# Two layers' adaLN modulation moved from VectorE, ScalarE and GpSimd to TensorE, ahead of the feed-forward stage

## The chip, the cores and the metric

The kernel runs on one core of a Trainium2 chip (trn2). The metric is the device time of one execution in microseconds (us), the median of several runs. The engines are TensorE (PE in the rows; PEld are its weight loads), VectorE (DVE), ScalarE (ACT), GpSimd (POOL) and SyncE (SP), which here only issues DMAs.

## What is computed

A first block (x is 256 tokens by 1024) mixes a gated delta rule with a dilated attention and has a gated feed-forward; a second block has two layers of attention and a mixture of 16 experts, each modulated by adaLN. All is float32. What the change touches is the modulation:

```python
def second_block(x, c, ada_w, ada_b, ...):
    silu_c = jax.nn.silu(c)                       # c: [1, 1024]
    for i in range(2):
        mod = silu_c @ ada_w[i] + ada_b[i]        # ada_w[i]: [1024, 6144]
        sh1, sc1, g1, sh2, sc2, g2 = [m[:, None, :] for m in jnp.split(mod, 6, axis=-1)]
        h = rms_norm(x, norm_mix_g[i]) * (1.0 + sc1) + sh1
        ...
        x = x + g1 * y
        h = rms_norm(x, norm_ffn_g[i]) * (1.0 + sc2) + sh2
        x = x + g2 * grouped_moe(h, ...)
```

So each layer multiplies one row of 1024 by a matrix of 1024 by 6144: 25 MB of weights a layer, and every weight is used once. It depends on c alone and not on x.

## The kernel before

**Stages.** In program order: the input projection and the gated delta rule, with the dilated attention's projections and heads as filler (the first 180 us or so), the output projection `mix` (L993) and a norm; the feed-forward in 22 steps f of 128 features (L1069 on); the second block's first attention, its experts, the second attention, its experts.

**Products.** Most weights are split into two float32r halves (`subs`, L338; the split is L232: a cast on ScalarE, a subtraction on VectorE or GpSimd), and each product is three float32r matmuls (`feat`, L543, and `tok_half`, L559 to L561). The experts (L1544, L1581), the delta rule's small products (L917 for the doubling, 64 by 64 blocks; L959) and the modulation's sums are in plain float32; the trace shows each of these matmuls as two records.

**Weights.** They come in units of [128, 2048] float32 (1.05 MB) through SP's queue (`wload`, L287). They go in turn to the buffers of up to three rings: `wp` (4 units), `wp2` (3, opened at L1013, where the delta rule's activations were) and `wp3` (3, opened behind the feed-forward, L1111, where the modulation's buffers were).

**Modulation.** `ada_unit(n)` (L365) takes one of 48 units: half the rows of 512 columns. It loads the unit to one of two buffers `wa` (L369); VectorE multiplies three of the four blocks of 128 rows by the column of silu(c) and adds them up in `acc` (L376, L381), and the fourth goes over ScalarE (L378) and GpSimd (L379). After every second unit `ada_sum` (L387) sums `acc` over the partitions with four matmuls against 32 columns of ones (L393), one for each group of 32 output partitions, adds the bias for the gates (L396), copies the row out (L398) and writes it to DRAM. `ada_load`, `ada_finish` and `ada_gate` (L414 to L432) read it back in the feed-forward and later.

**Order.** Each engine works off its own queue in order. The scheduler of the framework sets that order from the program, its priorities and pinned places. Units of modulation are put in by hand: `fill` (L709) advances the filler by one step and the modulation by `more` units at some 30 places of the delta rule, and each feed-forward step takes `step` units more (L1066, L1086), so that 20 units lie before the feed-forward and 28 within it.

```python
    def fill(n=1, more=1.0):
        for _ in range(n):
            drained[0] += 1
            next(filler, None)
            ada(more)
```

Of the kernel before, what the change touches and what calls it, by code (L numbers as in the profile page):

```python
# [10 lines left out]
F32 = mybir.dt.float32  # L11
# [16 lines left out]
# columns of the packed per-partition parameters  # L28
# [7 lines left out]
# columns of the packed rows that every partition gets  # L36
ROW = {"alog": (0, 4), "dtb": (4, 8), "rb": (8, 24), "lam": (24, 280)}
NROW = 280
# columns of the shape constants
# [7 lines left out]
# the first block needs those up to here  # L47
# [3 lines left out]
def _constants():  # L51
# [23 lines left out]
    # negated bias of the merged dilated attention: [q, head, (previous block | own block) keys back to front]  # L75
# [8 lines left out]
    # one-hot T5 bucket of rel = key - query, for rel = 127 .. -384  # L84
# [9 lines left out]
def _pack(inp):  # L94
# [6 lines left out]
    def feat(w):  # L101
        """[D, n] -> units of two blocks of 128 columns, each [128, k, 128 columns]"""
        n = w.shape[1]
        return A(w.reshape(KD, 128, n // 256, 2, 128).transpose(2, 1, 3, 0, 4)).reshape(n // 256, 128, 2048)

    def tok(w):
        """[D, n] -> units of 512 columns and half the rows, each [128, 4 k, 512 columns]"""
        n = w.shape[1]
        return A(w.reshape(2, 4, 128, n // 512, 512).transpose(3, 0, 2, 1, 4)).reshape(n // 256, 128, 2048)
# [27 lines left out]
    o["ada_w"] = A(g["ada_w_2"].reshape(2, 2, 4, 128, 12, 512).transpose(0, 4, 1, 3, 2, 5)).reshape(48, 128, 2048)  # L137
# [19 lines left out]
class InOrder:  # L157
    """an engine whose instructions keep their order in the program"""
# [10 lines left out]
def tile_block(ctx: ExitStack, tc: tile.TileContext, a: dict, out: bass.AP, dbg=None):  # L169
# [60 lines left out]
    def split(h, l, i, eng=None):  # L230
        """i = h + l exactly, each of a float32r's width"""
        return A_.copy(h, i), (eng or V).tensor_tensor(l, i, h.bitcast(F32), op=ALU.subtract)  # L232
# [31 lines left out]
    # the tensor engine's clock rises while x is on its way  # L264
# [25 lines left out]
    def wpair(ap, n):  # L290
        """(e, i) -> the i-th 512 columns of a unit for one of two experts; the n-th unit of a layer also finds room where activations were"""
# [30 lines left out]
    def after(i, name):  # L322
        """i is issued behind an instruction of its engine"""
# [3 lines left out]
    # rooms for split halves: s of two tiles of their own, 8 of one where activations are not  # L327
# [10 lines left out]
    def subs(ap, w=None, pinned=False, by=None, behind=None):  # L338
        """a unit of weights, loaded now or already on its way, as two split halves"""
# [21 lines left out]
    csil = const.tile([128, 8], F32, name="csil")  # L361
    adar = [dr.tile([6 * D], F32, name=f"adar{l}") for l in range(2)]
    ada_acc, ada_sums = [None], []

    def ada_unit(n):  # L365
        """half the rows (four blocks) of 512 columns of a layer's modulation, every fourth block on GpSimd"""
        l, s, u = n // 24, n // 2 % 12, n % 2
        w = adap.tile([128, 2048], F32, tag="wa", name="wa", bufs=2)
        nc.sync.dma_start(w, a["ada_w"][n])  # L369
        if u == 0:  # L370
            ada_acc[0] = adap.tile([128, 512], F32, tag="acc", name="acc", bufs=3)
        acc = ada_acc[0]
        for i in range(4):
            wi, k = w[:, i * 512:(i + 1) * 512], 4 * u + i
            if k == 0:
                V.tensor_scalar(acc, wi, csil[:, k:k + 1], None, op0=ALU.mult)  # L376
            elif i == 3:
                A_.activation(wi, wi, AF.Copy, scale=csil[:, k:k + 1])  # L378
                G.tensor_tensor(acc, acc, wi, op=ALU.add)  # L379
            else:  # L380
                V.scalar_tensor_tensor(acc, wi, csil[:, k:k + 1], acc, op0=ALU.mult, op1=ALU.add)  # L381
        if u == 1:
            if len(ada_sums) == 2:
                ada_sums.pop(0)()
            ada_sums.append(lambda: ada_sum(l, s, acc))

    def ada_sum(l, s, acc):  # L387
        """sum over partitions; with the bias for the gates, which are used as rows"""
        p = ps(128)
        gate = s // 2 in (2, 5)  # L390
        for j in range(4):
            o = p[32 * j:32 * j + 32, :]
            mm(o, ones[:, 0:32], acc[:, j * 128:(j + 1) * 128], start=True, stop=not gate)  # L393
            if gate:
                cb = P("adab")[:, l * 48 + s * 4 + j:l * 48 + s * 4 + j + 1]
                mm(o, cb.to_broadcast([128, 32]), ident, start=False, stop=True)  # L396
        sb = adap.tile([128, 128], F32, tag="adasb", name="adasb", bufs=3)
        A_.copy(sb, p)  # L398
        nc.scalar.dma_start(adar[l][s * 512:(s + 1) * 512].rearrange("(j c) -> j c", j=4),
# [5 lines left out]
    def ada(n):  # L405
        """n units more, fractions carried"""
# [12 lines left out]
    def ada_finish(l, t):  # L419
        """shift and scale as columns (the gates, used as rows, have the bias already)"""  # L420
# [15 lines left out]
    def warm(*waits):  # L436
        """holds the tensor engine's clock up through waits; nothing reads the products"""
# [5 lines left out]
    def rsq(o, i, scale):  # L443
        """o = (i * scale + eps) ** -0.5 through the activation tables"""
# [10 lines left out]
    def norm_rows(update=None, column_major=False, between=None, scaled=True):  # L455
        """x after update(b, c) of its [block, half row] pieces, and the rows of x over their root mean square"""
# [1254 lines left out]
```

## Time and profile before

| what | value |
|---|---|
| runs (3) | 1168.49, 1169.7, 1181.19 us |
| median | 1169.7 us |
| profiled execution, first to last instruction (span) | 1168.8 us |
| TensorE, VectorE, ScalarE, GpSimd busy in the span | 1091.2, 668.5, 467.4, 202.3 us |
| HBM read | 347.40 MB, 298 GB/s over the span |

The page gives the profiled execution's time as its span alone; the median of the runs is 0.9 us above it. The records of matmuls overlap one another, since matmuls are pipelined: the distance between two starts says what one costs, its own length does not. The granted clock stands in the stretches as a share of 2.4 GHz.

### The profile page before, as it was taken

Reading aid. Unit: us, or ns where it says so; the run is one execution under the profiler, and the core shown is the slowest. Engines: PE = TensorE matmul, PEld = TensorE weight load, DVE = VectorE, ACT = ScalarE, POOL = GpSimd, SP = SyncE. Lnnn points to the kernel's source line nnn. Section 1 sums busy time; section 2 is a strip of 40 time slices with the busy share of each in tenths; the row PEclk is TensorE's granted clock in tenths of the full one; section 3 lists DMA queues with packets and bytes.
Section 4 is the critical chain, followed back from the end, with each engine's and each line's share of the span. In section 5 each row is a group of like instructions: output and inputs, shape, how many; then the busy total and the mean of one; then the engine's idle time right before and its main releaser. Section 6 shows DMA issues by size and latency. Waiting matters only on the chain. (4 is left out here: it accounts for less than half of the span.)

```text
span 1168.8 us, 16805 instructions
## 1 busy us (share of the span) xinstructions
PE 1091.2 (93%) x6428; PEld 713.0 (61%) x6428; DVE 668.5 (57%) x1283; ACT 467.4 (40%) x942; POOL 202.3 (17%) x156
## 2 busy tenths in 40 slices
PE   8978889899999989999899998898999899999798
PEld 6957677788898868787334434236876544443332
DVE  6999987899999866777322212026656723221212
ACT  5763365655555565667211112016555511110200
POOL 2245543133123242001000000004221100000000
PEclk9999979899999999999999999899999989999999
DMA  8664766777877965356888999998653679899995
GB/s 323 253 252 182 264 246 223 284 285 279 338 284 311 369 247 177 135 200 221 333 349 343 418 422 423 406 421 316 191 184 144 254 305 372 327 424 424 422 419 203
DMA packets 53083, 349.75 MB, mean 299 GB/s; under 512 B 6392, under 2 KB 7192, under 8 KB 13056
## 3 DMA queue, kind: packets, MB, share of 16 engines
q1 hardware_dynamic: 50288, 342.51, 75.2%
q0 software_dynamic: 1792, 5.62, 1.7%
q8 instruction: 55, 0.90, 0.3%
q10 hardware_dynamic: 912, 0.43, 0.1%
q14 instruction: 36, 0.29, 0.1%
HBM read 347.40 MB, written 1.14 MB: 298 GB/s over the span
## 5 line engine op out<-in xcount | busy, mean ns | idle before, releaser
L1544 PE MATMUL pb<-w,XT 128*64 128x512 f32 x864 | 200.1, 609 | 10.3 <-PEq L1504 10.3
L232 DVE TENSOR_TENSOR wl<-w,wh 128x1024 fp32r<-128x1024 f32 x110 | 141.7, 1292 | 40.5 <-ACT wh L232 34.8
L232 ACT CAST wh<-w 128x1024 fp32r<-128x1024 f32 x132 | 137.6, 1044 | 65.5 <-PE pa L560 45.9
L1544 PEld LDWEIGHTS pb<-w,XT 128*64 128x64 f32 x864 | 61.9, 140 | 128.2 <-issue 124.5
L379 POOL TENSOR_TENSOR acc<-acc,wa 128x512 f32<-128x512 f32 x48 | 78.1, 1627 | 204.1 <-DVE acc L381 132.9
L1563 DVE TENSOR_TENSOR he<-he,pb 128x512 f32<-128x512 f32 (+1 forms) x20 | 11.4, 580 | 175.7 <-PE pb L1544 175.7
L381 DVE SCALAR_TENSOR_TENSOR acc<-wa,csil,acc 128x512 f32<-128x512 f32 x120 | 104.0, 867 | 13.4 <-POOL acc L379 8.9
L1581 PE MATMUL pb<-w,heT 128*64 128x512 f32 x480 | 108.1, 597 | 1.5 <-ACT heT L222 1.5
L1562 ACT ACTIVATE he<-pb 128x512 f32<-128x512 f32 (+1 forms) x20 | 10.0, 512 | 209.3 <-PE pb L1544 209.3
L559 PE MATMUL pa<-wh,hh 128*128 128x512 f32 x224 | 91.0, 408 | 2.5 <-ACT hh L532 2.5
L560 PE MATMUL pa<-wh,hl 128*128 128x512 f32 x224 | 88.4, 395 | 3.0 <-POOL hl L530 1.7
L561 PE MATMUL pa<-wl,hh 128*128 128x512 f32 x224 | 88.4, 394 | 0.0
L232 POOL TENSOR_TENSOR wl<-w,wh 128x1024 fp32r<-128x1024 f32 x22 | 54.7, 2488 | 178.3 <-ACT wh L232 139.4
L1584 DVE SCALAR_TENSOR_TENSOR he<-pb,gsl,g 128x512 f32<-128x512 f32 x32 | 24.0, 751 | 96.9 <-PE pb L1581 96.8
L1581 PEld LDWEIGHTS pb<-w,heT 128*64 128x64 f32 x480 | 32.8, 137 | 64.6 <-issue 58.5
L543 PE MATMUL pb<-hh,whl 128*128 128x256 f32 x320 | 62.3, 288 | 0.9 <-DVE gate L1076 0.9
L232 ACT CAST yh<-he 128x512 fp32r<-128x512 f32 x30 | 18.5, 616 | 103.6 <-DVE he L1584 103.6
L378 ACT ACTIVATE wa<-wa,csil 128x512 f32<-128x512 f32 x48 | 34.6, 722 | 58.5 <-DMA wa<-in_ada_w 57.2
L543 PE MATMUL pb<-hh,wh 128*128 128x256 f32 x192 | 55.5, 289 | 1.1 <-DVE hl L236 1.1
L543 PE MATMUL pb<-hl,wh 128*128 128x256 f32 x192 | 55.4, 288 | 0.0
L543 PE MATMUL pb<-hh,wl 128*128 128x256 f32 x192 | 55.2, 288 | 0.0
L543 PEld LDWEIGHTS pb<-hh,whl 128*128 128x128 f32 x320 | 51.3, 192 | 4.0 <-issue 3.4
(455 smaller groups left out, 2352.4 us busy)
## 6 DMA issues: line engine op xcount, KB each, us to landing
w<-in_m_gu SPq DMA_DIRECT2D x108, 1024.0 KB
w<-in_m_dn SPq DMA_DIRECT2D x58, 1024.0 KB
wa<-in_ada_w SPq DMA_DIRECT2D x48, 1024.0 KB
w<-in_w_gu SPq DMA_DIRECT2D x22, 1024.0 KB
w<-in_a_qkv SPq DMA_DIRECT2D x12, 1024.0 KB
wx<-in_m_gu SPq DMA_DIRECT2D x12, 1024.0 KB
w<-in_b_qkv SPq DMA_DIRECT2D x12, 1024.0 KB
w<-in_w_dn SPq DMA_DIRECT2D x11, 1024.0 KB
```

The source lines that it names most:

```text
L232: return A_.copy(h, i), (eng or V).tensor_tensor(l, i, h.bitcast(F32), op=ALU.subtract)
L378: A_.activation(wi, wi, AF.Copy, scale=csil[:, k:k + 1])
L379: G.tensor_tensor(acc, acc, wi, op=ALU.add)
L381: V.scalar_tensor_tensor(acc, wi, csil[:, k:k + 1], acc, op0=ALU.mult, op1=ALU.add)
L543: mm(p, w[:, c], r[:, k, :], start=(n == 0), stop=(n == 3 * KD - 1))
L559: mm(p[b], hh_, wh[:, c], start=(k == k0), stop=False)
L560: mm(p[b], hl_, wh[:, c], start=False, stop=False)
L561: mm(p[b], hh_, wl[:, c], start=False, stop=((k + 1) % KD == k0))
L1544: mm(pu[i][64 * e:64 * e + 64, :], xt[k // 4][:, k % 4, c0 + 64 * e:c0 + 64 * e + 64], w(e, i), start=(k == 0), stop=(k == KD - 1))
L1563: V.tensor_tensor(he[:, cs], he[:, cs], pu[1][:, cs], op=ALU.mult)
L1581: pin(mm(pd[h][64 * e:64 * e + 64, :], heT[:, k, e, :], w(e, i), start=(k == 0), stop=(k == 3)))
L1584: V.scalar_tensor_tensor(he, pd[h], gsl, g2[:, h * 512:(h + 1) * 512], op0=ALU.mult, op1=ALU.mult)
```

## The change

The modulation becomes matmuls. A unit is now 128 rows of 2048 columns, loaded as two halves of 1024 columns into five buffers (together 20 KB a partition, before 16 KB and the accumulators). Four matmuls, one for each 512 columns, multiply it by silu(c) spread over 32 columns and write to the four groups of 32 partitions of one PSUM bank, where eight units add up. Then come the gates' biases, one copy on ScalarE and one write to DRAM for 2048 columns. `fill` takes 1.8 times as many units, all that are left are done at the end of the delta rule, and the feed-forward has none. The third ring `wp3` opens where the second one does, before the last half of `mix`. The host packs `ada_w` in the new layout. All other lines of the diff only drop comments.

```diff
-    o["ada_w"] = A(g["ada_w_2"].reshape(2, 2, 4, 128, 12, 512).transpose(0, 4, 1, 3, 2, 5)).reshape(48, 128, 2048)
+    o["ada_w"] = A(g["ada_w_2"].reshape(2, 8, 128, 3, 2048).transpose(0, 3, 1, 2, 4)).reshape(48, 128, 2048)
...
     def ada_unit(n):
-        l, s, u = n // 24, n // 2 % 12, n % 2
-        w = adap.tile([128, 2048], F32, tag="wa", name="wa", bufs=2)
-        nc.sync.dma_start(w, a["ada_w"][n])
-        if u == 0:
-            ada_acc[0] = adap.tile([128, 512], F32, tag="acc", name="acc", bufs=3)
-        acc = ada_acc[0]
-        for i in range(4):
-            wi, k = w[:, i * 512:(i + 1) * 512], 4 * u + i
-            if k == 0:
-                V.tensor_scalar(acc, wi, csil[:, k:k + 1], None, op0=ALU.mult)
-            elif i == 3:
-                A_.activation(wi, wi, AF.Copy, scale=csil[:, k:k + 1])
-                G.tensor_tensor(acc, acc, wi, op=ALU.add)
-            else:
-                V.scalar_tensor_tensor(acc, wi, csil[:, k:k + 1], acc, op0=ALU.mult, op1=ALU.add)
-        if u == 1:
-            if len(ada_sums) == 2:
-                ada_sums.pop(0)()
-            ada_sums.append(lambda: ada_sum(l, s, acc))
-
-    def ada_sum(l, s, acc):
-        p = ps(128)
-        gate = s // 2 in (2, 5)
+        l, s, k = n // 24, n // 8 % 3, n % 8
+        ws = [adap.tile([128, 1024], F32, tag="wa", name="wa", bufs=5) for _ in range(2)]
+        for i, w in enumerate(ws):
+            nc.sync.dma_start(w, a["ada_w"][n][:, i * 1024:(i + 1) * 1024])
+        if k == 0:
+            ada_acc[0] = ps(512, "pa")
+        p = ada_acc[0]
+        gates = [j for j in range(4) if (4 * s + j) // 2 in (2, 5)]
         for j in range(4):
-            o = p[32 * j:32 * j + 32, :]
-            mm(o, ones[:, 0:32], acc[:, j * 128:(j + 1) * 128], start=True, stop=not gate)
-            if gate:
-                cb = P("adab")[:, l * 48 + s * 4 + j:l * 48 + s * 4 + j + 1]
-                mm(o, cb.to_broadcast([128, 32]), ident, start=False, stop=True)
-        sb = adap.tile([128, 128], F32, tag="adasb", name="adasb", bufs=3)
+            mm(p[32 * j:32 * j + 32, :], csil[:, k:k + 1].to_broadcast([128, 32]), ws[j // 2][:, j % 2 * 512:j % 2 * 512 + 512],
+               start=(k == 0), stop=(k == KD - 1 and j not in gates))
+        if k < KD - 1:
+            return
+        for c in range(4):
+            for j in gates:
+                i = l * 48 + 16 * s + 4 * j + c
+                mm(p[32 * j:32 * j + 32, c * 128:(c + 1) * 128], P("adab")[:, i:i + 1].to_broadcast([128, 32]), ident,
+                   start=False, stop=(c == 3))
+        sb = adap.tile([128, 512], F32, tag="adarow", name="adarow", bufs=1)
         A_.copy(sb, p)
...
     def fill(n=1, more=1.0):
+        more *= 1.8
...
     while drained[0] < 30:
         fill(1, .2)
+    while ada_next[0] < 48:
+        ada(1)
...
     rings.append(ctx.enter_context(tc.tile_pool(name="wp2", bufs=3, reuse_waits="tile")))
+    ada_ctx.__exit__(None, None, None)
+    wp3 = ctx.enter_context(tc.tile_pool(name="wp3", bufs=3, side="right", reuse_waits="tile"))
+    rings.append(wp3)
     for _ in mix(0):
         pass
...
-    step = (48 - ada_due[0]) / (NFF - 3.5)
...
-        ada(step)
...
     down(*prev)
-    ada_ctx.__exit__(None, None, None)
-    wp3 = ctx.enter_context(tc.tile_pool(name="wp3", bufs=3, side="right", reuse_waits="tile"))
-    rings.append(wp3)
```

TensorE's queue at the fifth doubling level of the delta rule (`R`, `X`, `Y`, `os` are 64 by 64 blocks; `wh`, `wl`, `hh`, `hl` belong to the filler), in the kernel before:

```order
L559 MATMUL pa<-wh,hh 128x512
L560 MATMUL pa<-wh,hl 128x512
L561 MATMUL pa<-wl,hh 128x512
L917 MATMUL pb<-R,X 64x64 x16
L917 MATMUL pb<-X,R 64x64 x8
L393 MATMUL pb<-acc,ones 32x128
L396 MATMUL pb<-ident,prm 32x128
```

The same place in the changed kernel (`wa` holds the modulation's weights, `csil` silu(c); L907 is the old L917):

```order
L548 MATMUL pa<-wh,hh 128x512
L549 MATMUL pa<-wh,hl 128x512
L550 MATMUL pa<-wl,hh 128x512
L377 MATMUL pa<-wa,csil 32x512 x2
L907 MATMUL pb<-R,X 64x64 x3
L377 MATMUL pa<-wa,csil 32x512 x2
L907 MATMUL pb<-R,X 64x64 x13
L907 MATMUL pb<-X,R 64x64 x9
L377 MATMUL pa<-wa,csil 32x512 x2
L907 MATMUL pb<-X,R 64x64 x7
```

The sums of 128 columns give way to matmuls of 512 columns, in pairs between the doubling's own products.

TensorE's queue at the end of the delta rule, where its output `oo` is turned and the output projection begins, before:

```order
L1006 MATMUL pb<-ident,oo 128x128
L560 MATMUL pa<-wh,yl 128x512
L561 MATMUL pa<-wl,yh 128x512
L1006 MATMUL pb<-ident,oo 128x128 x3
L559 MATMUL pa<-wh,yh 128x512
```

And in the changed kernel, with some more of the projection (`yh`, `yl`) up to the last unit of modulation:

```order
L998 MATMUL pb<-ident,oo 128x128 x7
L377 MATMUL pa<-wa,csil 32x512 x12
L384 MATMUL pa<-ident,prm 32x128 x8
L377 MATMUL pa<-wa,csil 32x512 x2
L548 MATMUL pa<-wh,yh 128x512
L549 MATMUL pa<-wh,yl 128x512
L550 MATMUL pa<-wl,yh 128x512
...
L550 MATMUL pa<-wl,yh 128x512
L377 MATMUL pa<-wa,csil 32x512 x20
L384 MATMUL pa<-ident,prm 32x128 x8
L548 MATMUL pa<-wh,yh 128x512
```

A run of 12 and one of 20 modulation matmuls now stand between the delta rule and the bulk of the output projection.

SP's queue from the projections of the dilated attention (`w_v`, `w_z`) to the output projection (`w_out`) and the feed-forward (`w_gu`, `w_dn`), before:

```order
L287 DMA w<-in_w_out 128x2048
L369 DMA wa<-in_ada_w 128x2048 x2
L287 DMA w<-in_w_gu 128x2048
L369 DMA wa<-in_ada_w 128x2048 x2
L287 DMA w<-in_w_dn 128x2048
L369 DMA wa<-in_ada_w 128x2048 x5
L287 DMA w<-in_w_out 128x2048
```

And in the changed kernel (one load of `wa` is half a unit):

```order
L371 DMA wa<-in_ada_w 128x1024 x18
L287 DMA w<-in_w_z 128x2048
L371 DMA wa<-in_ada_w 128x1024 x14
L287 DMA w<-in_w_z 128x2048
L371 DMA wa<-in_ada_w 128x1024 x6
L287 DMA w<-in_w_out 128x2048
L371 DMA wa<-in_ada_w 128x1024 x51
L287 DMA w<-in_w_out 128x2048 x3
L287 DMA w<-in_w_gu 128x2048 x2
L287 DMA w<-in_w_dn 128x2048
```

Before, feed-forward weights were asked for between units of modulation; now all of the modulation stands ahead of three of the four units of `w_out` and of everything behind them.

## Rows read from the trace of the kernel before

**Rows 1.** Busy us, share of the span and instructions of each engine, whole run
```profile
PE 1091.2 (93%) x6428; PEld 713.0 (61%) x6428; DVE 668.5 (57%) x1283; ACT 467.4 (40%) x942; POOL 202.3 (17%) x156
```

**Rows 2.** start:end, length, busy PE PEld DVE ACT POOL, clock, DMA share, GB/s
```profile
30.00:60.00 30.00, 27.78 (x228) 27.22 (x227) 29.65 (x50) 22.85 (x32) 9.54 (x5) 1.00 0.68 252
60.00:90.00 30.00, 23.33 (x145) 18.20 (x144) 28.27 (x55) 19.61 (x31) 12.13 (x8) 1.00 0.63 241
90.00:120.00 30.00, 25.60 (x350) 21.45 (x349) 28.40 (x34) 10.87 (x19) 16.53 (x9) 1.00 0.57 205
120.00:150.00 30.00, 25.82 (x372) 20.69 (x372) 28.48 (x32) 10.07 (x15) 15.54 (x9) 1.00 0.75 271
150.00:180.00 30.00, 27.17 (x156) 21.73 (x156) 23.97 (x75) 19.14 (x58) 11.73 (x10) 0.77 0.67 246
180.00:210.00 30.00, 29.01 (x141) 21.84 (x140) 24.91 (x44) 13.78 (x28) 10.91 (x11) 1.00 0.70 245
150.00:170.00 20.00, 17.57 (x103) 14.84 (x103) 15.97 (x42) 12.75 (x33) 8.13 (x7) 0.66 0.63 236
240.00:420.00 180.00, 176.57 (x1339) 158.91 (x1338) 162.04 (x212) 95.39 (x154) 50.80 (x32) 1.00 0.82 310
450.00:540.00 90.00, 89.26 (x476) 72.77 (x475) 66.94 (x186) 60.38 (x174) 10.55 (x6) 1.00 0.49 172
570.00:780.00 210.00, 199.01 (x940) 79.83 (x940) 42.08 (x85) 28.86 (x51) 0.00 (x0) 0.98 0.97 397
```

**Rows 3.** TensorE and VectorE in order of time at a doubling level: start, us, what
```profile
111.10 0.39 PE L561 MATMUL pa<-wl,hh 128*128 128x512 f32 x1
113.37 0.80 PE L917 MATMUL pb<-R,X 64*64 64x64 f32 x20 [1.88 <-DVE R L927]
...
110.04 1.54 DVE L376 TENSOR_SCALAR acc<-wa,csil 128x512 f32<-128x512 f32 x1
111.50 1.21 DVE L232 TENSOR_TENSOR wl<-w,wh 128x1024 fp32r<-128x1024 f32 x1
112.64 0.68 DVE L927 COPY R<-pb 128x512 f32<-128x512 f32 x1
```

**Rows 4.** The modulation's own instructions by stretch: length, DVE, ACT, POOL busy
```profile
30.00:210.00 180.00, 67.95 (x66) 15.85 (x22) 33.13 (x22) 0.96 0.67 243
240.00:420.00 180.00, 58.27 (x76) 17.36 (x24) 44.99 (x26) 1.00 0.82 310
```

**Rows 5.** TensorE in order of time around narrow float32 matmuls; two records a matmul
```profile
281.34 0.39 PE L1062 MATMUL pa<-wh,ml 128*128 128x512 f32 x1
281.56 0.39 PE L1063 MATMUL pa<-wl,mh 128*128 128x512 f32 x1
281.88 0.43 PE L393 MATMUL pb<-acc,ones 128*32 128x128 f32 x8
282.24 0.39 PE L543 MATMUL pb<-hh,whl 128*128 128x256 f32 x1
...
549.74 0.86 PE L1318 MATMUL pa<-xT,rws 128*32 128x128 f32 x24
...
619.52 3.65 PE L1544 MATMUL pb<-w,XT 128*64 128x512 f32 x16
623.01 1.46 PE L1544 MATMUL pb<-wx,XT 128*64 128x512 f32 x6
```

**Rows 6.** A copy out of PSUM (ns min/median/max), then the groups of the two splits
```profile
L222 ACT COPY v<-pa x4: 586/586/587, 470.3 to 874.5; 128x512 f32<-128x512 f32 x4
...
L232 DVE TENSOR_TENSOR wl<-w,wh 128x1024 fp32r<-128x1024 f32 x110 | 141.7, 1292 | 40.5 <-ACT wh L232 34.8
L232 ACT CAST wh<-w 128x1024 fp32r<-128x1024 f32 x132 | 137.6, 1044 | 65.5 <-PE pa L560 45.9
```

**Rows 7.** SP's queue in order of time, first loads of the second block
```profile
389.56 53.86 SPq L287 DMA_DIRECT2D w<-in_a_qkv  x12
```

**Rows 8.** TensorE in order of time, first product of the feed-forward
```profile
219.71 0.58 PE L543 MATMUL pb<-hh,wh 128*128 128x256 f32 x1 [1.05 <-DVE hl L236]
```

More of the change, by code (lines that the diff above doesn't have):

```diff
@@ L362, in tile_block @@
     adar = [dr.tile([6 * D], F32, name=f"adar{l}") for l in range(2)]
-    ada_acc, ada_sums = [None], []
+    ada_acc = [None]
     def ada_unit(n):
-        l, s, u = n // 24, n // 2 % 12, n % 2
-        w = adap.tile([128, 2048], F32, tag="wa", name="wa", bufs=2)
-        nc.sync.dma_start(w, a["ada_w"][n])
-        if u == 0:
-            ada_acc[0] = adap.tile([128, 512], F32, tag="acc", name="acc", bufs=3)
-        acc = ada_acc[0]
-        for i in range(4):
-            wi, k = w[:, i * 512:(i + 1) * 512], 4 * u + i
-            if k == 0:
-                V.tensor_scalar(acc, wi, csil[:, k:k + 1], None, op0=ALU.mult)
-            elif i == 3:
-                A_.activation(wi, wi, AF.Copy, scale=csil[:, k:k + 1])
-                G.tensor_tensor(acc, acc, wi, op=ALU.add)
-            else:
-                V.scalar_tensor_tensor(acc, wi, csil[:, k:k + 1], acc, op0=ALU.mult, op1=ALU.add)
-        if u == 1:
-            if len(ada_sums) == 2:
-                ada_sums.pop(0)()
-            ada_sums.append(lambda: ada_sum(l, s, acc))
@@ L398, in ada_sum @@
+        if k < KD - 1:
[6 more added lines that the diff above has]
+        sb = adap.tile([128, 512], F32, tag="adarow", name="adarow", bufs=1)
         A_.copy(sb, p)
-        nc.scalar.dma_start(adar[l][s * 512:(s + 1) * 512].rearrange("(j c) -> j c", j=4),
+        nc.scalar.dma_start(adar[l][s * 2048:(s + 1) * 2048].rearrange("(j c) -> j c", j=4),
@@ L1096, in tile_block @@
         if f == 7:
-            assert ada_next[0] >= 30
             adat = ada_load(0)
@@ L1102, in tile_block @@
             g1 = ada_gate(0, 2)
-        if f == NFF - 3:
-            while ada_sums:
-                ada_sums.pop(0)()
-            assert ada_next[0] == 48
         if f == NFF - 1:
```

## The prediction

> **What bounds the kernel now.** I read the page's busy line first, then a table of stretches, then single instructions around the operations in question, and last the DMA queue. The chain of waits is of no use here: it only reaches back over the last 60 us, far behind the stages that change.
>
> The busy line names TensorE (93%) [rows 1]. An average over stages does not say which wait ends last, so the table of stretches comes next [rows 2]. Three things are to be seen in it. From 30 to 210 us (input projection, delta rule, dilated attention) TensorE and VectorE are both nearly full: VectorE at 28 to 30 of 30 us up to 150 us, TensorE at 23 to 29. From 240 to 420 us (feed-forward) TensorE is idle for 180 - 176.57 = 3.4 us in all. From 570 to 780 us (first mixture of experts) the DMA engines run at a share of 0.97 and 397 GB/s. So the stage in which the added matmuls land has little room on TensorE, and the question is how much.
>
> Its room from 30 to 210 us: the six rows leave 2.22 + 6.67 + 4.40 + 4.18 + 2.83 + 0.99 = 21.3 us idle. To that comes the clock: from 150 to 170 us the granted clock averages 0.66 [rows 2], a mixture of the two levels 1.2 and 2.4 GHz, behind a stretch with many small matmuls and waits; 20 x (1 - 0.66) = 6.8 us of full-speed work are lost. Together 28.1 us could be won at most if every wait there vanished. Those waits do hang on what the change removes: at 111.10 us TensorE begins its last filler matmul and starts the next doubling product at 113.37, idle 1.88 us until VectorE has copied R, and VectorE's queue shows why: a modulation instruction of 1.54 us and a subtraction of 1.21 us stand ahead of that copy [rows 3].
>
> **The change part by part.**
>
> *Removed.* The modulation leaves VectorE (68.0 us from 30 to 210, 58.3 from 240 to 420), ScalarE (15.9 and 17.4) and GpSimd (33.1 and 45.0) [rows 4]. None of that is time by itself: it counts only through TensorE's waits, above. Also removed are 24 sums over partitions. One such group (eight records, four matmuls on 32 columns each) starts at 281.88 behind a matmul that began at 281.56; the matmuls there follow each other at 0.22 us, so it was free to start at 281.78, and the next starts at 282.24: 0.46 us. 24 x 0.46 = 11.0 us, 16 of the 24 in the feed-forward [rows 5]. The bias products of the gates stay, 32 as before; they only move.
>
> *Added on TensorE.* 48 units of four matmuls, moving 512 columns of float32 against a 32-column weight. The trace has no such form, so I take it from two rows. A 512-column float32 product on 64 columns: sixteen records, eight matmuls two by two, start at 619.52 and the next ones at 623.01, so 0.87 us for a round of two side by side. That four of 32 columns also run side by side is to be seen where one group of eight records spans 0.43 us and three groups span 0.86: 0.215 us more for each group of four [rows 5]. So a round of up to four is 0.87 us. The order on TensorE has 59 runs (39 of two matmuls, 9 of four, 4 of eight, 2 of one, 2 of three, one each of 6, 12 and 20), and a run of n needs n/4 rounds, rounded up: 70 rounds. 70 x 0.87 = 60.9 us. That half the units are cut into pairs costs 22 rounds beyond the 48.
>
> Each run also pays for going in and out of the 32-column form: 0.46 - 0.215 = 0.245 us from the same group of sums. 59 x 0.245 = 14.5 us. Bounds: not below the 0.10 us visible ahead of the group (5.9 us), not above 0.245. I take the upper end, since the row is of the same form.
> The Trainium skill, page "TensorEngine Tiling (Array Packing)", section "Key Properties", says that changing the tiling mode drains TensorE, while changing only the tile does not; it gives no price. The 0.245 us agrees with it in place and sign, and without any drain the forecast would be 14.5 us lower, 1197.
>
> *Waits on TensorE that go.* Of the 28.1 us I take 26: in the new order a run of modulation matmuls stands in front of nearly every product that waited. Bounds 14 and 28.1. In the feed-forward 3.4 us are idle up to 420 us, and some more in its first and last steps; I take 4, bounds 2 and 5.
>
> *Moved: the loads.* All 96 half units (0.52 MB each) now go through SP's queue ahead of the last three units of w_out and of every feed-forward weight. Each waits for one of five buffers, so for a run on TensorE, and everything behind it on SP waits too. Up to the end of the delta rule this costs nothing: the order wants 148 of the 192 matmuls, 74 halves or 39 MB, by then, which at the 397 GB/s that the DMA engines reach from 570 to 780 us [rows 2] is 98 us of a stage of about 180. The tail differs: the last 44 matmuls need 22 halves, five are on hand, 17 x 1.32 us = 22 us, about what TensorE needs for them (14 rounds, 8 runs and 24 products of the projection at 0.22 us: 19.5 us); I take 4 us for the unevenness of a run of 20. Then comes a new wait: ScalarE copies the last accumulator (0.59 us, as a copy of that size in [rows 6]) only when that run has ended, and behind it in ScalarE's queue stand seven casts of w_out halves. One cast and one subtraction, 1.04 + 1.29 us [rows 6], and their hand-overs pass before TensorE gets on: 4 us more. Together 8 us, bounds 3 and 16. The accumulator's PSUM bank is inside this wait.
>
> *Moved: the buffers.* The third weight ring opens before the feed-forward instead of behind it. I cost that at nothing: the second block's first weights are asked for at 389.56 us already, while the feed-forward still runs [rows 7], and from 450 to 540 us TensorE is busy 89.26 of 90 us with the DMA engines half idle [rows 2]. Without that cover a unit that comes late by one transfer would cost 1.05 MB at 397 GB/s, 2.6 us. The mixture of experts has the same bytes and buffers as before.
>
> *Sum.* 60.9 + 14.5 - 11 - 26 - 4 + 8 = +42 us, of which about +53 stand before the feed-forward and -11 in it. Against the profiled execution's span of 1168.8 us that is 1210.8; the median of the runs lies 0.9 above the span, so 1212.
> Own range: the best ends, 60.9 + 5.9 - 11 - 28.1 - 5 + 3 = +25.7, give 1195; the worst, 60.9 + 14.5 - 11 - 14 - 2 + 16 = +64, give 1234.
>
> **The rivals.**
>
> *Pairs beside their neighbours (not slower).* A run of one or two uses only 64 of the 128 output columns. If it ran beside narrow neighbours, such as the 64 by 64 products of the doubling, 41 runs x 1.1 us = 45 us would vanish: 42 - 45 = -3, so 1167. From 30 hidden runs on, the result is within 1%. For it: column groups do run side by side [rows 5]. Against: most neighbours in the order are 128 columns wide, and the group of sums was entered and left with a gap on both sides.
>
> *TensorE has more slack than its busy time shows.* Pipelined matmuls look busy while they wait. The weight loads fill only 131.1 of the 180 us from 30 to 210 [rows 2], 48.9 us free. If all of that took work: 60.9 + 14.5 - 11 - 48.9 - 6.8 - 4 + 8 = +12.7, 1182. Against: float32 products load few weights while they stream for long, and there are many here.
> The Trainium skill, page "Perfetto Trace Analysis", section "Identifying the Most-Contended Engine", tells to judge TensorE's room by the busy share of its weight loads and not by that of its matmuls; by that rule this rival is the forecast.
>
> *The queue feeds too slowly.* From 30 us on, 57 units of 1.05 MB (48 of modulation, 9 of projections) must come up to the last half, 59.8 MB. At 271 GB/s, the best 30 us of this stage [rows 2], they end 221 us later, at 251, some 12 us after TensorE would want them: 1224. Against: that rate was set by buffers, not by the engines (share 0.75).
>
> *Four column groups do not share a round at 512 columns.* Two rounds for each four: 28 rounds more, +24, 1236. Against it stand the sums in [rows 5].
>
> **How the numbers follow.** Forecast 0.72; queue 0.10; slack 0.08; pairs beside neighbours 0.05; no sharing 0.05. A measurement of this kernel tells about 1% (12 us) from no change. Slower by over 1%: 0.72 + 0.10 + 0.05 and a quarter of the slack's 0.08, 0.89. Within 1%: the rest of the slack and half of the pairs, 0.08. Faster: 0.03. The predicted time is 1212; the range 1186 to 1236 takes in the own range, the queue case, the case without sharing and the upper part of the slack case.
>
> **What would show it.** The first feed-forward product starts at 219.7 us now [rows 8]; it should start near 273. The added matmuls should show 0.87 us for a round of two or of four alike, and some 0.2 us around each run. VectorE should be busy for half of the time or less from 60 to 150 us, while TensorE's idle time from 30 to 210 falls below 5 us, and the granted clock should stay at its upper level there. The feed-forward should take some 11 us less. Wrong would be a round well under 0.87 us, a feed-forward that begins before 250 us, or a gain that appears only behind 430 us.

## The result and the profile after

The changed kernel takes 1227.7 us (1223.5 to 1230.6), the kernel before 1169.4: a ratio of 1.0469, 95% interval 1.0418 to 1.0519. It is slower, as forecast; the forecast of 1212 us was 16 us short, its range reached to 1236.

The profiled execution has a span of 1228.7 us. The busy line of its page, the answer to [rows 1]:

```profile
PE 1164.6 (95%) x6620; PEld 724.3 (59%) x6620; DVE 542.5 (44%) x1139; ACT 436.9 (36%) x874; POOL 119.7 (10%) x108
```

TensorE is busier by 73 us, while VectorE lost 126 us and GpSimd 83. The stretches (columns as in [rows 2]):

```profile
30.00:60.00 30.00, 30.00 (x248) 28.70 (x246) 29.54 (x57) 22.36 (x30) 8.39 (x4) 1.00 0.67 244
60.00:90.00 30.00, 29.92 (x164) 15.44 (x163) 10.15 (x22) 14.02 (x24) 5.66 (x4) 1.00 0.88 304
90.00:120.00 30.00, 29.21 (x282) 19.56 (x282) 13.80 (x32) 5.91 (x11) 6.22 (x4) 1.00 0.79 266
120.00:150.00 30.00, 30.00 (x360) 19.42 (x359) 8.88 (x11) 6.30 (x7) 6.10 (x4) 1.00 0.88 299
150.00:180.00 30.00, 29.77 (x271) 15.96 (x269) 8.22 (x14) 7.63 (x10) 2.39 (x3) 1.00 0.80 264
180.00:210.00 30.00, 29.98 (x171) 16.48 (x170) 13.86 (x59) 11.62 (x47) 2.32 (x2) 1.00 0.66 219
210.00:230.00 20.00, 16.72 (x81) 6.28 (x81) 7.28 (x24) 5.03 (x15) 3.60 (x7) 0.91 0.87 277
230.00:260.00 30.00, 25.26 (x124) 8.01 (x122) 0.00 (x0) 0.59 (x1) 0.00 (x0) 0.94 0.92 331
260.00:290.00 30.00, 23.98 (x100) 17.14 (x97) 14.02 (x15) 11.42 (x18) 8.16 (x5) 0.89 0.99 414
```

Up to 210 us TensorE is now idle 1.1 us where it was 21.3, at the full clock throughout, and VectorE has 33 of 90 us of work from 60 to 150 us where it had 85. Behind 210 us come stretches that have no counterpart before: TensorE idle 3 to 6 us in each, the clock lower, VectorE with nothing to do from 230 to 260, and the DMA engines at a share of 0.87 to 0.99.

The first product of the feed-forward, the answer to [rows 8], and its last one in each kernel (TensorE in order of time):

```profile
292.22 0.58 PE L532 MATMUL pb<-hh,wh 128*128 128x256 f32 x1 [1.46 <-DVE hl L236]
...
481.63 0.39 PE L1058 MATMUL pa<-wl,mh 128*128 128x512 f32 x1
```

```profile
424.32 0.39 PE L1063 MATMUL pa<-wl,mh 128*128 128x512 f32 x1
```

So the feed-forward starts 72.5 us later (292.2 for 219.7) and takes 15.2 us less (189.8 for 205.0); what follows it takes 2.6 us more.

The added matmuls cost what was worked out. TensorE around a run of four (eight records), then the last runs of modulation and the output projection behind them:

```profile
206.34 0.27 PE L609 MATMUL pb<-ident,pt 128*128 128x128 f32 x1
206.54 1.06 PE L377 MATMUL pa<-wa,csil 128*32 128x512 f32 x8
207.54 0.65 PE L615 MATMUL pb<-ptT,vb 128*64 128x256 f32 x2
...
244.11 0.40 PE L549 MATMUL pa<-wh,yl 128*128 128x512 f32 x1
244.43 1.05 PE L377 MATMUL pa<-wa,csil 128*32 128x512 f32 x4
245.42 0.50 PE L550 MATMUL pa<-wl,yh 128*128 128x512 f32 x1
245.85 1.91 PE L377 MATMUL pa<-wa,csil 128*32 128x512 f32 x12
248.37 1.05 PE L377 MATMUL pa<-wa,csil 128*32 128x512 f32 x4 [0.61 <-DMA wa<-in_ada_w]
250.78 1.05 PE L377 MATMUL pa<-wa,csil 128*32 128x512 f32 x4 [1.35 <-DMA wa<-in_ada_w]
252.42 4.21 PE L377 MATMUL pa<-wa,csil 128*32 128x512 f32 x12 [0.59 <-DMA wa<-in_ada_w]
257.19 1.05 PE L377 MATMUL pa<-wa,csil 128*32 128x512 f32 x4 [0.56 <-DMA wa<-in_ada_w]
258.48 1.05 PE L377 MATMUL pa<-wa,csil 128*32 128x512 f32 x4 [0.24 <-DMA wa<-in_ada_w]
259.36 1.04 PE L384 MATMUL pa<-ident,prm 128*32 128x128 f32 x16
262.70 0.55 PE L548 MATMUL pa<-wh,yh 128*128 128x512 f32 x1 [2.31 <-ACT wh L232]
263.05 0.63 PE L549 MATMUL pa<-wh,yl 128*128 128x512 f32 x1
265.14 0.79 PE L550 MATMUL pa<-wl,yh 128*128 128x512 f32 x1 [1.47 <-POOL wl L232]
```

A run of four holds TensorE from 206.54 to 207.54 and a run of two from 244.43 to 245.42: 1.00 and 0.99 us for twice the columns. Runs of several rounds add 0.86 us each, so this is one round of 0.86 and 0.12 us behind it. Ahead of the run of two stand 0.32 us instead of the 0.23 to which neighbours keep: a mode change costs some 0.2 us. The run of 20 that begins at 245.85 needs five rounds, 4.3 us, and lasts 13.5 us up to its biases at 259.36; each gap ends with a DMA. The gaps add up to 3.4 us only. Behind the first six matmuls a half lands at a time, and its two matmuls go alone: the last 14 matmuls take seven rounds in place of three or four. The rest is the lower clock. After the run TensorE waits 2.31 us for ScalarE's cast and 1.47 us for GpSimd's subtraction.

What SP's queue waited for from 30 to 210 us (its line, whose end it waited for, us in all, times, longest us). For 112.5 of the 180 us a load of the modulation stood at its head until TensorE had worked off a buffer:

```profile
SPq L371 <- PE pa L377: 112.5, 46, 7.2
```

Summed over the trace, the modulation's matmuls (without the biases) hold TensorE for 87.1 us. 70 rounds of 0.857 are 60.0 of them. Of the other 27.1 us, 21.4 stand in seven of the 58 runs, and there almost all is due to weights that come late: 5.1 at 218.1 us, 2.8 at 226.7, 9.2 at 245.8, the rest in four small ones. Less 0.12 us for each of these runs that is 20.5 us, called waits for weights from here on. For 9.0 us TensorE is idle in the runs; the rest is halves that land apart and so cost a round each, and rounds at the lower clock.

### The profile page after: what moved, and what is told of

It is laid out like the page before. It is cut to its first block, busy times and chain, and to the rows that moved or that the text cites. A ratio compares the mean times of both kernels' runs of the same rounds, so it can differ in the third digit from the quotient of the medians.

```text
span 1228.7 us, 16876 instructions
## 1 busy us (share of the span) xinstructions
PE 1164.6 (95%) x6620; PEld 724.3 (59%) x6620; DVE 542.5 (44%) x1139; ACT 436.9 (36%) x874; POOL 119.7 (10%) x108
## 5 line engine op out<-in xcount | busy, mean ns | idle before, releaser
L232 DVE TENSOR_TENSOR wl<-w,wh 128x1024 fp32r<-128x1024 f32 x110 | 136.0, 1238 | 121.2 <-ACT wh L232 110.2
L377 PE MATMUL pa<-wa,csil 128*32 128x512 f32 x384 | 84.8, 619 | 9.1 <-DMA wa<-in_ada_w 9.0
L232 ACT CAST yh<-he 128x512 fp32r<-128x512 f32 x30 | 18.5, 617 | 103.6 <-DVE he L1569 103.6
L548 PEld LDWEIGHTS pa<-wh,hh 128*128 128x128 f32 x224 | 42.1, 189 | 13.4 <-ACT hh L521 3.4
L549 PEld LDWEIGHTS pa<-wh,hl 128*128 128x128 f32 x224 | 42.5, 190 | 12.5 <-DVE hl L522 2.2
```

Source lines behind the costliest of these rows:

```text
L377: mm(p[32 * j:32 * j + 32, :], csil[:, k:k + 1].to_broadcast([128, 32]), ws[j // 2][:, j % 2 * 512:j % 2 * 512 + 512], start=(k == 0), sto ...
L548: mm(p[b], hh_, wh[:, c], start=(k == k0), stop=False)
L549: mm(p[b], hl_, wh[:, c], start=False, stop=False)
```

## The experiments

Times up to the feed-forward's end, read from each trace (us), and what was measured. "Projection" is the start of the last output projection product, "FF" the first feed-forward product's start and the last one's end:

| kernel | projection | FF first | FF end | median | ratio, 95% interval |
|---|---|---|---|---|---|
| before | 210.3 | 219.7 | 424.7 | 1169.4 | 1 |
| changed | 283.0 | 292.2 | 482.0 | 1227.7 | 1.0469, 1.0418 to 1.0519 |
| e1_cols64 | 264.4 | 273.5 | 462.4 | 1207.2 | 1.0326, 1.0303 to 1.0348 |
| e2_noload | 226.5 | 235.9 | 425.3 | see text | see text |
| e3_whole | 260.4 | 269.7 | 458.8 | 1202.5 | 1.0299, 1.0261 to 1.0337 |
| e4_relief | 186.9 | 196.1 | 395.5 | 1139.6 | 0.9730, 0.9704 to 0.9755 |
| e5_whole24 | 271.7 | 280.8 | 471.0 | 1215.3 | 1.0358, 1.0288 to 1.0427 |
| e6_hybrid | 206.4 | 216.6 | 413.2 | 1156.7 | 0.9873, 0.9812 to 0.9935 |
| e7_pool2d | 216.7 | 229.3 | 439.3 | 1186.5 | 1.0125, 1.0062 to 1.0189 |
| e8_pool2 | 218.1 | 230.8 | 457.0 | 1199.4 | 1.0247, 1.0178 to 1.0316 |
| e9_h16 | 201.1 | 213.0 | 417.4 | 1165.7 | 0.9967, 0.9929 to 1.0006 |
| e10_h16i | 200.0 | 209.1 | 414.0 | 1160.2 | 0.9924, 0.9900 to 0.9948 |
| e11_h8i | 206.7 | 215.9 | 420.6 | 1163.8 | 0.9932, 0.9900 to 0.9963 |
| e12_hybrid5 | 205.0 | 215.2 | 411.8 | 1157.3 | 0.9890, 0.9871 to 0.9908 |

**TensorE's rounds or the loads? e1, e2, e3.**

```diff
-            mm(p[32 * j:32 * j + 32, :], ..., ws[j // 2][:, j % 2 * 512:j % 2 * 512 + 512],
+            n_ = 512 if k == 0 else 64
+            mm(p[32 * j:32 * j + 32, 0:n_], ..., ws[j // 2][:, j % 2 * 512:j % 2 * 512 + n_],
```

> The changed kernel, with the modulation's matmuls on 64 of their 512 columns in all units but the first of each group of eight (seven eighths of the modulation's product is left out in those; loads, waits and order stay). Theory A, TensorE pays for the rounds: 42 of 48 units' share of 70 rounds, 61 rounds, get shorter by 7/8 of 0.857 us = 0.75 us, 46 us in all; some of it is given back as waits for the loads in the tail, so 1185 us (1178 to 1200). Theory B, the loads bind the whole stage: the matmuls only fill time in which TensorE would wait for weights, so 1215 us or more.

Between the two. The order did not stay as it was: the scheduler put the last 64 matmuls together, where the changed kernel has at most 20. The delta rule ended as early as in the kernel before (its last output turned from 186.9 us on, before 188.6), but then stood a run of 64 matmuls with its biases, from 188.9 to 239.8 us. TensorE in order of time in it (64 columns but for each first unit), and that stretch (columns as in [rows 2]):

```profile
203.79 0.43 PE L378 MATMUL pa<-wa,csil 128*32 128x64 f32 x4 [0.85 <-DMA wa<-in_ada_w]
205.07 0.42 PE L378 MATMUL pa<-wa,csil 128*32 128x64 f32 x4 [0.85 <-DMA wa<-in_ada_w]
206.35 0.42 PE L378 MATMUL pa<-wa,csil 128*32 128x64 f32 x4 [0.85 <-DMA wa<-in_ada_w]
...
190.00:240.00 50.00, 16.80 (x153) 8.25 (x154) 1.04 (x3) 2.47 (x4) 0.00 (x0) 0.58 1.02 374
```

Every half waits for its own load, one each 1.28 us, with the DMA engines at a share of 1.02. However little TensorE does in this order, the last weights come at 235 us. That is a floor under the stage which the sum did not have.

```diff
-        ws = [adap.tile([128, 1024], F32, tag="wa", name="wa", bufs=5) for _ in range(2)]
-        for i, w in enumerate(ws):
-            nc.sync.dma_start(w, a["ada_w"][n][:, i * 1024:(i + 1) * 1024])
+        if n == 0:
+            kept_ws[:] = [adap.tile([128, 1024], F32, tag=f"wa{i}", name="wa", bufs=1) for i in range(2)]
+            for i, w in enumerate(kept_ws):
+                nc.sync.dma_start(w, a["ada_w"][n][:, i * 1024:(i + 1) * 1024])
+        ws = kept_ws
```

> The changed kernel, with every unit's matmuls reading the one unit that is loaded first (47 of the 48 units' weights are left out; the matmuls and their order stay). Theory A: only the waits for modulation weights go, 26 us as summed over the runs of modulation matmuls, most of them in the runs at 218, 227 and 246 us, so 1201 us (1195 to 1207); the restart behind the last run stays. Theory B, the loads bind the whole stage: 45 us or more go, under 1185. Theory C, the waits in the tail are hidden by something else that is late as well (the output projection's weights): 1220 or more.

Its time (3076.5 us) says nothing: with other modulation the tokens go to other experts, and behind the feed-forward come 2652 us where the others have 740 to 747. Up to there it can be read, and the feed-forward ends 56.7 us earlier than in the changed kernel. By the number that is theory B's, but not by its reason: without loads to wait for, the scheduler put the halves together, 28 runs and 50 rounds for 58 and 70. That makes 20 x 0.857 + 30 x 0.22 = 23.7 us. The rest, 33.0 us, is nearly made up by the waits for weights (20.5 us, where the expectation had 26), the restart behind them (2.31 + 1.47 us) and the lower clock: over the three stretches from 210 to 290 us, 20 x 0.09 + 30 x 0.06 + 30 x 0.11 = 6.9 us, of which a part is counted in the waits already. The run that was 9.2 us late goes through here without a gap (TensorE, 61 records, between the biases):

```profile
196.41 7.03 PE L379 MATMUL pa<-wa,csil 128*32 128x512 f32 x61
```

The run did not separate the two effects as planned; the next one does.

```diff
-        ws = [adap.tile([128, 1024], F32, tag="wa", name="wa", bufs=5) for _ in range(2)]
-        for i, w in enumerate(ws):
-            nc.sync.dma_start(w, a["ada_w"][n][:, i * 1024:(i + 1) * 1024])
+        w = adap.tile([128, 2048], F32, tag="wa", name="wa", bufs=2)
+        nc.sync.dma_start(w, a["ada_w"][n])
+        ws = [w[:, 0:1024], w[:, 1024:2048]]
```

> The changed kernel, with each unit loaded in one piece of 2048 columns (8 KB a row) to two buffers, in place of two halves of 1024 columns to five. Theory A: a round costs the same with two or four matmuls, so 70 rounds become 48, 22 x 0.857 = 18.9 us, and some 13 mode changes of 0.22 us go, 2.9 us: 1206 us (1196 to 1212), with fewer matmuls in 2-wide runs. Theory B, buffers and loads bind: four halves' worth of buffers in place of five make the waits longer, 1225 or more.

Theory A, 1202.5 for 1206: 44 runs and 49 rounds in its trace. It agrees with the price of a round, and shows that cutting units in pairs cost over 20 us (halves that land apart are gone with them). And with as many rounds as the kernel without loads it reaches the end of the projection 33.9 us later; 16 mode changes are 3.5 of them, so the loads, with what they bring along, cost some 30 us here too: from 30 us to the projection's end TensorE is idle for 18.7 us and loses some 12 to the clock (0.95 on average), without loads 0.9 and none. The last run of 20 (16 matmuls, biases, 4 more) shows it: its first 16 matmuls take 13.7 us (208.15 to the biases at 221.89) for 3.4 us of rounds, and from 210 to 260 us the clock averages 0.85 (TensorE, then that stretch with the columns of [rows 2]):

```profile
208.15 1.94 PE L377 MATMUL pa<-wa,csil 128*32 128x512 f32 x8 [5.14 <-DMA wa<-in_ada_w]
212.08 1.94 PE L377 MATMUL pa<-wa,csil 128*32 128x512 f32 x8 [1.99 <-DMA wa<-in_ada_w]
217.69 1.93 PE L377 MATMUL pa<-wa,csil 128*32 128x512 f32 x8 [3.68 <-DMA wa<-in_ada_w]
220.19 1.93 PE L377 MATMUL pa<-wa,csil 128*32 128x512 f32 x8 [0.56 <-DMA wa<-in_ada_w]
...
210.00:260.00 50.00, 40.27 (x217) 20.96 (x214) 6.44 (x8) 7.65 (x11) 2.37 (x1) 0.85 0.93 355
```

**Asked for earlier: e5.**

```diff
-        more *= 1.8
+        more *= 2.4
```

> The changed kernel with whole units in two buffers, as in the run before of that form (1202.5 us), and 2.4 units of modulation asked for at each step of the filler in place of 1.8. Theory A, the loads are fed too late: the run of 20 matmuls that took 18.5 us there for 4.3 us of rounds holds the loss because too many units are left for the end; asked for earlier they come while the DMA engines have room (shares 0.66 to 0.88 from 30 to 210 us in the changed kernel), so 1193 us (1188 to 1198). Theory B, the stage moves its bytes as fast as two buffers let it: the waits only move from the tail to the runs ahead of it, 1200 to 1207.

Worse than both: 1215.3. The last modulation starts at 246.3 us instead of 253.3, but the run of 20 with its biases still lasts 18.9 us (18.5 there), the delta rule's output is turned 11 us later (212.8 for 201.9), and of the projection's 96 products, which had filled gaps between the runs, 72 now stand behind the last one (26 in e3). Theory A falls. The loads are not late because they are asked for late; asked for sooner, they hold up the delta rule.

**What VectorE's relief is worth: e4.**

```diff
-            elif i == 3:
-                A_.activation(wi, wi, AF.Copy, scale=csil[:, k:k + 1])
-                G.tensor_tensor(acc, acc, wi, op=ALU.add)
-            else:
-                V.scalar_tensor_tensor(acc, wi, csil[:, k:k + 1], acc, op0=ALU.mult, op1=ALU.add)
+            elif k == 4:
+                V.scalar_tensor_tensor(acc[:, 0:64], wi[:, 0:64], csil[:, k:k + 1], acc[:, 0:64], op0=ALU.mult, op1=ALU.add)
```

> The kernel before, without the modulation's multiply-adds on VectorE, ScalarE and GpSimd beyond the first block of each group and 64 columns of the fifth (most of the modulation's product is left out; loads and sums over partitions stay). It prices by itself what the relief of VectorE is worth to TensorE. Theory A: the waits of 30 to 210 us go, 26 us of 28.1, and 4 us in the feed-forward: 1139 us (1135 to 1146). Theory C: TensorE's idle time there passes to other waits (ScalarE's casts, the delta rule's chain): 1152 or more.

Theory A, to the microsecond: 23.4 us at the end of the projection and 5.6 in the feed-forward. Its stretches from 60 to 150 us (columns as in [rows 2]) leave TensorE 3.0 us idle where it had 15.3:

```profile
60.00:90.00 30.00, 29.34 (x256) 25.37 (x255) 23.70 (x53) 18.60 (x34) 9.08 (x7) 1.00 0.71 271
90.00:120.00 30.00, 29.84 (x430) 23.88 (x430) 17.38 (x23) 8.30 (x11) 9.57 (x6) 1.00 0.86 324
120.00:150.00 30.00, 27.80 (x278) 23.35 (x273) 16.62 (x46) 13.22 (x34) 3.72 (x3) 0.83 0.83 308
```

So taking nearly all of the modulation off VectorE is worth 30 us; the clock of 0.83 in the last stretch, which costs 5 us, stays. Against that and the sums' 11 us stand 48 rounds of 0.857, 41.1 us, and 0.22 for each run, 51.7 us if every unit is a run of its own. Only with all units in a few long runs could all 48 about break even, before any wait for a load.

**Relief from elsewhere: e7, e8.** In both, the kernel before with `elif i >= 2` for `elif i == 3` (e7: for the first 28 units). The expectation takes these 28 for the ones ahead of the feed-forward, but 28 is the number that the program places within it; by the trace of the kernel before some 22 units are ahead of it (22 instructions of ScalarE from 30 to 210 us in [rows 4]).

> The kernel before with two of the four blocks of a unit, in place of one, on ScalarE and GpSimd for the 28 units ahead of the feed-forward. It takes 28 multiply-adds of 0.75 us (21 us) off VectorE and adds 0.72 us each to ScalarE and 1.29 us each to GpSimd, without a cycle of TensorE. Theory A, VectorE's load is what TensorE waits for: a third of the relief measured with nearly all of it gone (23 us at the end of the output projection), so 1162 us (1158 to 1167). Theory C, the waits pass to GpSimd's sums, behind which VectorE's next multiply-add stands: 1168 or more.

> As the run with two blocks on ScalarE and GpSimd, but in all 48 units, those of the feed-forward too. Theory A: another 2 us in the feed-forward, where the relief of all of it was worth 6 us: 1160 us (1156 to 1166). Theory C: GpSimd, with 24 to 28 us more in the feed-forward, holds the sums back, 1168 or more.

Theory C in both, by the time. In e7 VectorE's multiply-adds wait three times as long for GpSimd's sums as the 8.9 us of the kernel before (what VectorE's line waited for, e7):

```profile
L381 DVE SCALAR_TENSOR_TENSOR acc<-wa,csil,acc x92: 733/746/2907, 43.4 to 413.3; 128x512 f32<-128x512 f32 x92
...
  POOL acc L379: 26.3, 14
```

From 30 to 210 us VectorE loses 18 us of work, yet TensorE is idle 22.1 us and its clock averages 0.91 (before: 21.3 and 0.96). So its waits stayed, and what makes the projection 6.4 us later is the clock: 0.05 of 180 us, 9 us. A queue is not only as long as its work: in this stretch VectorE's blocks waited 16.8 us for GpSimd's sums, before 4.2. That these waits also brought the clock down was not shown.

**Half on TensorE: e6, and again e12.** The first layer's units take the changed kernel's way (whole units, two buffers), the second layer's that of the kernel before:

```diff
     def ada_unit(n):
+        if n < 24:
+            return ada_unit_pe(n)
         l, s, u = n // 24, n // 2 % 12, n % 2
```

> The kernel before with the first layer's 24 units as whole units on TensorE in the delta rule, and the second layer's 24 as before on VectorE, ScalarE and GpSimd. Theory A, price and relief are both in proportion to the units: 24 rounds of 0.857 us and 23 runs with a mode change of 0.22 us cost 25.6 us, against 24/28 of the 23 us that the relief was worth at the end of the output projection and 6 sums of 0.46 us fewer: 1169 us (1164 to 1175), no change that can be told. Theory D, the relief comes mostly from the first units that leave VectorE: 1160 or less. Theory B, any weight on TensorE in that stage waits for its load: 1178 or more.

> The run with the first layer's 24 units on TensorE and the second layer's 24 as before, again with five rounds, for a narrower interval (before: 0.9873, 0.9812 to 0.9935). Theory D, most of VectorE's relief comes from the units that leave it first, inside the delta rule, while the loads keep their old pace: a ratio of 0.985 to 0.991, below the 0.9924 of 16 units in turn. If the first result was chance, 0.992 or more.

It beats both kernels, the one before by 1.1%: 1156.7 and 1157.3 us, the second ratio 0.9890 (0.9871 to 0.9908). Theory D. Stretches of e6 (columns as in [rows 2]):

```profile
60.00:90.00 30.00, 28.67 (x196) 20.64 (x195) 17.30 (x46) 15.88 (x28) 6.84 (x5) 1.00 0.81 300
90.00:120.00 30.00, 30.00 (x386) 23.04 (x385) 11.03 (x15) 7.08 (x12) 8.52 (x5) 1.00 0.66 235
120.00:150.00 30.00, 30.00 (x384) 20.79 (x383) 11.74 (x17) 8.08 (x9) 7.16 (x5) 1.00 0.81 309
150.00:180.00 30.00, 29.09 (x180) 19.02 (x179) 16.65 (x73) 17.17 (x61) 5.92 (x9) 1.00 0.67 231
```

Half the units give nearly all the relief (idle 2.6 us from 30 to 210 us, clock 1.00). The reason lies in where units stand: some 22 of the kernel before's stood in the stage whose waits cost TensorE time, and in e6 VectorE's first modulation starts at 226.2 us, behind the projection:

```profile
L406 DVE TENSOR_SCALAR acc<-wa,csil x12: 472/480/1523, 226.2 to 376.9; 128x512 f32<-128x512 f32 x12
```

So these 24 units clear that stage altogether, and the share of 24/28 in theory A was a miscount. With the other 24 left for the feed-forward the loads have no tail: the 25 runs of modulation take 28.1 us for 27 rounds of 0.857, 23.1 us. The projection ends 3.9 us earlier than before and the feed-forward takes 8.4 us less. Four sums fewer explain 1.8 of the 8.4. Another 4.5 or so are TensorE's waits and clock in the feed-forward: idle 3.4 us at a clock of 0.99 before, 0.9 at 1.00 in e6 (TensorE busy 201.57 of 205.0 and 195.68 of 196.6 us). Some 2 us are open.

**Fewer than half: e9, e10, e11.** A list gives each unit its way: 16 units first on TensorE, then 8 on VectorE (e9); two and one in turn (e10); one and two in turn, 8 on TensorE (e11).

The list of e10, and the lines below it against e6:

```diff
+ADA = [v for i in range(8) for v in ((1, 0, i // 4, 2 * i % 8), (1, 0, i // 4, 2 * i % 8 + 1), (0, 0, 8 + i // 2, i % 2))] + ...
-        if n < 24:
-            return ada_unit_pe(n)
-        l, s, u = n // 24, n // 2 % 12, n % 2
+        pe, l, s, u = ADA[n]
+        if pe:
+            return ada_unit_pe(n, l, s, u)
```

> The kernel before with 16 of the first layer's units as whole units on TensorE, asked for first, and its last 8 units and the second layer as before on VectorE, ScalarE and GpSimd. In the run with 24 on TensorE it is idle only 2.6 us from 30 to 210 us and VectorE half free from 90 to 150. Theory A, TensorE has been freed of its waits and now every unit on it costs its price: 8 rounds of 0.857 us and 8 mode changes of 0.22 us fewer, 4 sums of 0.46 us more, 1150 us (1146 to 1154). Theory E, the waits on VectorE come back as units return to it: 1156 or more.

> As the run with 16 units on TensorE, but two units on TensorE and one on VectorE in turn, so that VectorE's eight units do not come together behind 140 us. Theory A: as there or up to 3 us better, 1148 us (1144 to 1153). Theory E, VectorE's units hurt where the doubling's copies stand, from 90 to 150 us: 1156 or more.

> As the run with units in turn, but 8 on TensorE and 16 of the first layer on VectorE, one to two. Theory A with waits only at a full VectorE: 16 rounds and mode changes (17.2 us) fewer than with 24 on TensorE, 8 sums (3.7 us) more, and waits on VectorE back for a half of what the 24 took away, some 10 us: 1153 us (1146 to 1160). Theory E, relief in proportion: two thirds of the way back to the kernel before, 1165.

Theory A misses in e9 and e10; e11 lies between the two, at theory E's end. The projection does end 4 to 6 us earlier with 16 units than in e6 and e12, as theory A has it, but the feed-forward takes 8 us longer again (204.4 and 204.9 for 196.6), so the sum is no better: e9 loses clearly, while the intervals of e10 and e12 overlap. TensorE's waits and clock in the feed-forward hold some 5 of the 8 us: idle 2.3 us at a clock of 0.98 in e9, 4.7 us at 0.99 in e10. Waits for ScalarE's `mh` are 2.2 and 2.6 us of that. In e9 the price is also seen where its eight units come together (columns as in [rows 2]), with VectorE nearly full up to 180 us and the clock lower:

```profile
150.00:180.00 30.00, 26.08 (x147) 20.20 (x145) 26.56 (x84) 19.66 (x67) 11.06 (x13) 0.94 0.48 146
180.00:210.00 30.00, 25.99 (x115) 19.03 (x113) 19.69 (x32) 12.65 (x21) 9.29 (x6) 0.95 0.92 342
```

## Why the prediction was right, and where it fell short

*Price of a round: right.* 0.857 us for 0.87, alike for two and four matmuls, 70 rounds. e3 took 21 of them away and won 25 us for a forecast of 22.

*Mode change: right in place, a little high.* At most 0.22 us for 0.245, 58 runs: up to 12.8 us for 14.5. The gaps ahead of and behind the runs (0.10 and 0.12 us) agree with the drain that the Trainium skill, page "TensorEngine Tiling (Array Packing)", section "Key Properties", states without a price.

*Waits that go: right.* 26 us forecast; the changed kernel has 1.1 us idle left of 21.3 and none of the 6.8 us lost to the clock, and e4 shows 23.4 us for the relief by itself.

*Feed-forward: right.* -15.2 us for -11; e4's 5.6 us and 16 sums of 0.46 us make 13.0.

*The tail: the term that was mis-sized.* "Together 8 us, bounds 3 and 16." The waits for weights measured 20.5 us, the restart behind the last run 3.8, and up to 6.9 went to the lower clock from 210 to 290 us: 24 to 31 us, 16 to 23 more than forecast and beyond the upper bound. Up to the feed-forward +53 were forecast and +72.5 measured, 19 more, so this one term holds nearly the whole difference. Two steps failed. "Up to the end of the delta rule this costs nothing" rests on "39 MB ... at the 397 GB/s ... is 98 us of a stage of about 180": it took the rate of another stage, and counted the modulation's bytes alone. In the changed kernel the DMA engines moved 219 to 304 GB/s per stretch up to 210 us, since SP's queue stood 112.5 us waiting for TensorE to give a buffer free, and some 9 of the 20.5 us fall before 226 us, where the delta rule's output is turned. Behind it, 22 us of loads were to lie beside 19.5 us of TensorE's work, with 4 us for unevenness. The loads did not lie beside it: 12 us of waits came on top, with halves landing one by one. The restart by itself was as forecast. That the time missed by 16 us and not by 19 is luck: the feed-forward gained 4 us more than forecast.

*The rivals.* Slow feeding, given 0.10 and 1224 us, named the mechanism that made up the difference; e2 and e3 put the loads at some 30 us in all, where the rival added 12 to the 8 of the tail. Pairs hidden beside neighbours and groups that don't share a round are both excluded by the 0.99 and 1.00 us above. Slack behind busy TensorE is excluded by e3 and e1 together: fewer rounds were paid back, in e1 up to the floor of the loads. The busy share of weight loads, by which the Trainium skill, page "Perfetto Trace Analysis", section "Identifying the Most-Contended Engine", judges TensorE's room, misleads for these products: weight loads fill 115.6 of the 180 us from 30 to 210 in the changed kernel, and still each round costs its full time. The same section of the Trainium skill names the share of peak arithmetic beside it, which was not worked out here.

*What stays open.* Why the clock fell in the tail was not tried; TensorE had waited there for weights, and that much alone the rows show. Nor is it shown why ScalarE's `mh` comes late in the feed-forward of e9 and e10 and not in that of e6, with 23 or 24 of VectorE's units in it each time.

## What to carry to other kernels

Before work moves from a full engine to the one that sets the pace, price the relief by itself by leaving the work out (here 30 us, and 11 us of sums) and set it against the price on the other side (here 41 us of rounds and up to 11 us of mode changes): these two decide before any arrangement does. Then move only the work that stands where the waits are: here the 24 units that cleared the delta rule of it brought nearly all the relief, and the others, from a stage with 3.4 us of waits, only their cost. And work that carries its own weights takes along its loads: add up all bytes that must land before the stage's end, at the rate that this stage's buffers reach, not that of the best stage.

## What was not expected of the hardware

Loads of half a unit came one each 1.28 us in e1 (0.524 MB in rows of 4 KB, 410 GB/s) with TensorE waiting for each; over that stretch of 50 us the mean was 374 GB/s at a share of 1.02. Where TensorE mostly waited there (busy 16.8 of 50 us), its granted clock averaged 0.58, between the levels of 1.2 and 2.4 GHz, and nearer to the lower; the first products of the projection behind it follow each other at 0.43 us instead of 0.22.
